# Weight transfers of one unit in five buffers, and the low part of a unit in one operation

## The chip, the cores and the metric

The kernel runs on one core of a Trainium2 chip. The metric is the device time of one execution in microseconds. The kernel before took 2624.03 us, the median of three runs (2620.69 to 2626.52).

## The reference

Two layers of a hybrid block over 256 tokens of width 2048, in float32. In each layer, with `h` the residual stream:

```python
u = rms_norm(h, mix_pre_g[l])
proj = u @ w_in[l]                        # 2048 x 4352, in layer 1 also w_in_vres
y_rwkv = rwkv7_time_mix(...)              # 16 heads of 64, a scan over the tokens
y_mla = mla_heads(...)                    # 8 heads, w_uq (512 x 1536), w_ukv (256 x 2048)
y = concatenate([y_rwkv, y_mla]) @ w_out[l]
h = h + rms_norm(y, mix_post_g[l])
y = memory_cross_attention(rms_norm(h, mem_pre_g[l]), mem_n, wq, wk, wv, wo)
h = h + rms_norm(y, mem_post_g[l])
y = square(relu(rms_norm(h, ffn_pre_g[l]) @ w_ff1[l])) @ w_ff2[l]   # 2048 x 8192 and back
h = h + rms_norm(y, ffn_post_g[l])
```

Every weight is used once for all 256 tokens, so each one passes from HBM to the core once.

## The kernel before

Matmuls with the big weights take both operands as a high and a low part: the high part is the value cast to TensorE's 32-bit matmul format (fp32r), the low part is the value minus the high part. A product is three matmuls: high x high, high x low, low x high (`go`, L309, and the same in `gemmB`, L360).

A *unit* is the piece of a weight that is split at once: 512 KB for 512 columns, two k-tiles of 128 rows (`per = 2`), or four k-tiles for up to 256 columns (`per = 4`). Its way has these steps:

1. **Transfer.** SP's queue issues the transfer from HBM into a tile of the pool `rawp` (L148), which has two buffers. `units` (L258) takes two units in one transfer of up to 1 MB. `hunits` (L280), for the weights of the attention projections, where columns of several heads are picked out, takes a whole slice of 2 or 4 k-tiles into one buffer, one transfer of 256 KB for each k-tile. A buffer comes free when the low parts of all its units are done, and SP issues its transfers in order.
2. **High part.** ScalarE casts the unit (L298), into a ring of four buffers (`ring`, L149), or, where `heap` says so, into the larger pool `heap4`.
3. **Low part.** VectorE subtracts (L300 or L304). While `ffn_on` is set (the two FFNs, from the second of their eight blocks of hidden columns on) this is one operation for a unit (L300); elsewhere it is two, one for each half of the unit's k-tiles (L304).
4. **Use.** TensorE reads both. A ring buffer comes free after its last matmul.

The first units of all (`first`, in the small projection of layer 0) are an exception: the first two have a transfer and a buffer in `heap4` each, and the pairs in `rawp` begin after them.

The matmul loops take the units from generators: `gemmA` (tokens as the stationary operand, weights moving) and `gemmB` (weights stationary) are one unit ahead of TensorE in the program, `gemm_seq` follows an order that is written out. The last product of each FFN goes through `gemm_seq`: all units of the third column block for the first 128 tokens, then the same units for the other 128, then the fourth block in the same way, whose units are split into `heap4`.

TensorE's order is the program's own: between the matmuls of the big products, small generators (`spawn`, `poll`, `wait`) add the matmuls of the scan, of attention and of the transposes, by a running clock with fixed delays. The other engines' queues are ordered by the planner of the framework, which also sets all semaphores. So a cast for a weight stands in ScalarE's queue between copies from PSUM, squares and exponentials, and a subtraction in VectorE's between the operations of the scan.

Names in the profile: `raw` is a transferred tile, `wh` and `wl` the two parts, `uh`/`ul` the split activations, `hdh`/`hdl` the hidden layer of the FFN, `qn`, `kn`, `qrT` copies in the attention projections, `rf` and `rl` the FFN's activations.

Of the kernel before, what the change touches and what calls it, by code (L numbers as in the profile page):

```python
# [9 lines left out]
F32 = mybir.dt.float32  # L10
F32R = mybir.dt.float32r
AF = mybir.ActivationFunctionType
ALU = mybir.AluOpType
# [3 lines left out]
NK = 16  # L17
# [116 lines left out]
class K:  # L134
# [1 line left out]

    def __init__(self, tc, I, out, ctx, n4=24, n2=18, nring=4, nraw=2):
        self.tc, self.nc, self.I, self.out = tc, tc.nc, I, out  # L140
        self.n = 0
        self.clk, self.fib, self.evt = 0.0, [], {}
        E = ctx.enter_context
        PS = bass.MemoryType.PSUM
        self.cp = E(tc.tile_pool(name="cp", bufs=1))
        self.heap = E(tc.tile_pool(name="heap", bufs=n2))
        self.heap4 = E(tc.tile_pool(name="heap4", bufs=n4))
        self.rawp = E(tc.tile_pool(name="rawp", bufs=nraw))  # L148
        self.ring = E(tc.tile_pool(name="ring", bufs=nring))  # L149
        self.tp = E(tc.tile_pool(name="tp", bufs=8))  # L150
        self.sp = E(tc.tile_pool(name="sp", bufs=16))
        self.gp = E(tc.tile_pool(name="gps", bufs=4, space=PS))
        self.xp = E(tc.tile_pool(name="xps", bufs=4, space=PS))
        self.dr = E(tc.tile_pool(name="drp", bufs=1, space=bass.MemoryType.DRAM))
        nc = self.nc
        self.Id = self.cp.tile([128, 128], F32, name="Id")
        self.V = self.cp.tile([128, L, NV], F32, name="V")
        self.C = self.cp.tile([128, NC_ - 128], F32, name="C")
        self.mhalf = self.cp.tile([128, 16], F32, name="mhalf")
        nc.gpsimd.memset(self.mhalf, -0.5)  # L160
        self.ident = self.Id
# [93 lines left out]
        g.tensor_tensor(out=dst, in0=t, in1=self.mhalf[:, : src.shape[-1]], op=ALU.pow)  # L255


    def units(self, src, k0, nk, ncols, extra=None, heap=None, first=False):  # L258

        nc = self.nc  # L260
        per = 4 if ncols <= 256 else 2
        ks = range(k0, k0 + nk, 2 * per)
        if first:
            ks = [k0, k0 + per, *ks[1:]]
        for ka, kb in zip(ks, [*ks[1:], k0 + nk]):
            kn = kb - ka
            if first and kn == per:
                raw = self.t4("raw", [128, kn, ncols])
            else:
                raw = self.rawp.tile([128, kn, ncols], F32, tag="raw", name=self.nm("raw"))  # L270
            rows = slice(ka * 128, (ka + kn) * 128)
            n0 = src.shape[1]
            nc.sync.dma_start(out=raw[:, :, :n0], in_=src[rows, :].rearrange("(k p) n -> p k n", p=128))
            if extra is not None:
                nc.sync.dma_start(out=raw[:, :, n0:], in_=extra[rows, :].rearrange("(k p) n -> p k n", p=128))
            for j in range(0, kn, per):
                i = (ka + j - k0) // per
                yield self.split(raw[:, j : j + per, :], per, ncols, heap is not None and i >= heap) + (list(range(ka + j, ka + j + per)),)

    def hunits(self, w, nk, h0, nh, dh, hw, off):  # L280

        nc = self.nc
        raw = self.rawp.tile([128, nk, nh, dh], F32, tag="raw", name=self.nm("raw"))
        wv = w.rearrange("(k p) (h c) -> k p h c", p=128, c=hw)
        for k in range(nk):
            nc.sync.dma_start(out=raw[:, k], in_=wv[k, :, h0 : h0 + nh, off : off + dh])
        rv = raw.rearrange("p k h d -> p k (h d)")
        for j in range(0, nk, 2):
            yield self.split(rv[:, j : j + 2, :], 2, nh * dh) + ([j, j + 1],)

    def split(self, raw, per, ncols, heap=False):
        nc = self.nc
        if heap:
            wh, wl = (self.t4(s, [128, per, ncols], F32R) for s in ("wh", "wl"))
        else:
            wh = self.ring.tile([128, per, ncols], F32R, tag="wh", name=self.nm("wh"))
            wl = self.ring.tile([128, per, ncols], F32R, tag="wl", name=self.nm("wl"))
        nc.scalar.copy(out=wh, in_=raw)  # L298
        if self.ffn_on:
            nc.vector.tensor_tensor(out=wl, in0=raw, in1=wh.bitcast(F32), op=ALU.subtract)  # L300
        else:
            for j in range(0, per, per // 2):
                s = slice(j, j + per // 2)
                nc.vector.tensor_tensor(out=wl[:, s], in0=raw[:, s], in1=wh[:, s].bitcast(F32), op=ALU.subtract)  # L304
        return wh, wl

    ffn_on = False

    def go(self, o, x, wh, wl, start, stop):  # L309
        xh, xl = x  # L310
# [222 lines left out]

    def small_units(self, l):
        w = self.I["w_in"][l]
        return self.units(w[:, 3072:3520], 0, NK, 448 + (64 if l else 0), extra=self.I["w_in_vres"][l - 1] if l else None, heap=4, first=l == 0)

    def small(self, l, U, rstd, units):
        nc, I = self.nc, self.I
# [803 lines left out]
    def ffn(self, l, U, rstd, done, ff):  # L1343
        nc, I = self.nc, self.I
        w1, w2 = I["w_ff1"][l], I["w_ff2"][l]
        rhs = self.rhsU(U)
        y = None
        part = [self.sm("fp", [128, 4]) for _ in range(2)]
        gb = None
        NB = 8  # L1350

        def ff1(b):
            H = ([], [])
            for j in range(2):
                hh, hl = self.newU(4, "hd")
                c0 = b * 1024 + j * 512
                if b == 0 and j == 0:
                    self.ff1_first(l, ff, U, hh[0], hl[0])
                else:
                    def ev(q, ps, hh=hh[0], hl=hl[0]):  # L1360
                        r = self.t2("rl", [128, 2, 256])
                        nc.scalar.activation(out=r, in_=ps, func=AF.Relu)  # L1362
                        nc.gpsimd.tensor_tensor(out=r, in0=r, in1=r, op=ALU.mult)  # L1363
                        o = hh[:, 2 * q : 2 * q + 2, :]
                        nc.scalar.copy(out=o, in_=r)  # L1365
                        nc.vector.tensor_tensor(out=hl[:, 2 * q : 2 * q + 2, :], in0=r, in1=o.bitcast(F32), op=ALU.subtract)  # L1366

                    self.gemmB(self.units(w1[:, c0 : c0 + 512], 0, NK, 512), NK, rhs, ev)
                H[0].extend(hh)
                H[1].extend(hl)  # L1370
            return H

        def ff2(b, H, gb):
            lh = self.lhsU(H)
            lhs = lambda k, t: lh(k - 8 * b, t)

            def ev(n):
                def f(t, ps):
                    o = y[t][n]
                    if b == 0:  # L1380
                        nc.scalar.activation(out=o, in_=ps, func=AF.Copy, scale=s2[t])
                    else:
                        nc.vector.scalar_tensor_tensor(out=o, in0=ps, scalar=s2[t], in1=o, op0=ALU.mult, op1=ALU.add)  # L1383
                    if b == NB - 1:
                        junk = self.t2("junk", [128, 512])
                        nc.scalar.activation(out=junk, in_=o, func=AF.Square, accum_out=part[t][:, n : n + 1])
                        y[t][n] = self.t2("yg", [128, 512])
                        nc.vector.tensor_tensor(out=y[t][n], in0=o, in1=gb[n], op=ALU.mult)
                        if n == 3:
                            done(t, y, part)  # L1390
                return f

            un = lambda n, heap=None: self.units(w2[:, n * 512 : (n + 1) * 512], 8 * b, 8, 512, heap=heap)
            last = b == NB - 1
            for n in range(2 if last else 4):
                self.gemmA([un(n)], 8, lhs, 512, ev(n))
            if last:
                self.gemm_seq([(un(2), 8, 512, ev(2)), (un(3, 0), 8, 512, ev(3))], lhs,
                              [(0, 0, 4), (0, 1, 4), (1, 0, 4), (1, 1, 4)])

        H = ff1(0)
        y = self.tiles4()
        s2 = [self.sm("s2", [128, 1]) for _ in range(2)]
        for t in range(2):
            nc.gpsimd.tensor_tensor(out=s2[t], in0=rstd[t], in1=rstd[t], op=ALU.mult)
        self.ffn_on = True
        for b in range(NB):
            Hn = ff1(b + 1) if b + 1 < NB else None
            if b == NB - 1:
                gb = self.load_bc(I["ffn_post_g"][l])  # L1410
            ff2(b, H, gb)
            H = Hn
        self.ffn_on = False


    def load_h(self, h, src, q, t, cols=range(4)):
# [100 lines left out]
```

## Time and profile before

| | before |
|---|---|
| median of 3 runs, us | 2624.03 |
| profiled execution, us | 2620.89 |
| its span, us | 2619.1 |
| granted TensorE clock, mean | 0.989 |
| TensorE matmuls busy, us | 2528.3 (97%) |
| VectorE busy, us | 1593.2 (61%) |
| ScalarE busy, us | 1205.2 (46%) |
| GpSimd busy, us | 435.4 (17%) |
| moved by DMA | 456.69 MB, 174 GB/s in the mean |

The span goes from the first to the last instruction. A matmul's end is modelled, and matmuls overlap, so TensorE counts as busy while any of them is under way. "Idle before, releaser" in a row is the time for which an engine did nothing before an instruction, and what ended that. L273 and the like are lines of the kernel; PE is TensorE, DVE VectorE, ACT ScalarE, POOL GpSimd, SP the queue that issues the weights' transfers. PEclk is the granted TensorE clock as a share of full speed.

In time the span has: the start and the mixing stage of layer 0 (projections, scan, attention, w_out) to about 445 us, memory attention to about 570, the FFN to about 1300, then the same for layer 1.

### The profile page before, as it was taken

To read this page: it belongs to the slowest core of one execution; us is meant where nothing else is said; L and a number is where in the kernel's file an instruction comes from. 1 tells how busy PE (TensorE), PEld (TensorE's weight loads), DVE (VectorE), ACT (ScalarE), POOL (GpSimd) and SP (SyncE) were. 2 spreads that over 40 slices of the span, in tenths; PEclk is the share of its full clock that TensorE was granted. 3 is DMA by queue.
4 is the path that set the end of the run, shared out by engine and by line. 5 is a ranking of instruction groups with operands and counts; after the bars stand their busy time and mean duration, and the time that the engine had idled before them with its cause. 6 is when DMAs were issued, how large, how long until landed. Compare 5 with 4: busy or idle time off the path is not lost.

```text
span 2619.1 us, 42411 instructions
## 1 busy us (share of the span) xinstructions
PE 2528.3 (97%) x17458; PEld 2280.7 (87%) x17458; DVE 1593.2 (61%) x2445; ACT 1205.2 (46%) x1724; POOL 435.4 (17%) x597
## 2 busy tenths in 40 slices
PE   8999999999999999999999998999999999999997
PEld 7989878979899899989788887789798998899896
DVE  4786876675445555555667778757754545555555
ACT  5454555544444444444454544545544444444443
POOL 2323414211000000000034245202100000000000
PEclk9999999999999999999999999999999999999999
DMA  5444536645555555555554444365455555555554
GB/s 201 153 150 132 156 123 207 206 129 178 192 181 190 193 188 183 191 195 193 194 167 154 143 132 149 114 233 190 129 177 193 182 189 193 186 184 193 188 198 145
DMA packets 250850, 456.69 MB, mean 174 GB/s; under 512 B 19268, under 2 KB 52420, under 8 KB 250656
## 3 DMA queue, kind: packets, MB, share of 16 engines
q1 hardware_dynamic: 241280, 422.77, 49.3%
q0 software_dynamic: 9376, 31.21, 3.6%
q8 instruction: 137, 2.24, 0.4%
q14 instruction: 57, 0.47, 0.1%
HBM read 444.50 MB, written 9.44 MB: 173 GB/s over the span
## 4 chain that ended last, share of the span: by engine, by line
PE 65%; issue 12%; DVE 10%; DMA 7%; ACT 3%; POOL 3%; SPq 0%; ACTq 0%; DVEq 0%; POOLq 0%
PE g L243 57%; PE x L243 7%; DVE wl L304 3%; DMA raw<-in_w_ff_dram 2%; ACT wh L298 2%; DMA raw<-in_w_in_dram 1%; PE x L248 1%; DMA raw<-in_w_out_dram 1%; DVE h L469 1%; DVE wl L300 1%; DVE uf L411 1%; DMA raw<-in_wk_mem_dram 1%; DMA raw<-in_wq_mem_dram 1%; DVE T L784 0%; DVE fs L782 0%
## 5 line engine op out<-in xcount | busy, mean ns | idle before, releaser
L298 ACT CAST wh<-raw 128x1024 fp32r<-128x1024 f32 (+2 forms) x804 | 832.0, 1042 | 1043.3 <-PE g L243 690.4
L300 DVE TENSOR_TENSOR wl<-raw,wh 128x1024 fp32r<-128x1024 f32 x480 | 586.1, 1223 | 570.7 <-ACT wh L298 567.8
L243 PE MATMUL g<-uh,wh 128*128 128x256 f32 x2816 | 807.1, 287 | 0.7 <-ACT wh L298 0.7
L243 PE MATMUL g<-uh,wl 128*128 128x256 f32 x2816 | 796.9, 283 | 1.2 <-DVE wl L304 1.2
L243 PE MATMUL g<-ul,wh 128*128 128x256 f32 x2816 | 796.6, 283 | 0.0
L304 DVE TENSOR_TENSOR wl<-raw,wh 128x512 fp32r<-128x512 f32 (+2 forms) x648 | 433.0, 709 | 193.1 <-ACT wh L298 192.2
L243 PEld LDWEIGHTS g<-uh,wh 128*128 128x128 f32 x2816 | 539.9, 192 | 6.2 <-issue 2.3
L243 PEld LDWEIGHTS g<-uh,wl 128*128 128x128 f32 x2816 | 540.2, 192 | 4.2 <-DVE wl L304 2.0
L243 PEld LDWEIGHTS g<-ul,wh 128*128 128x128 f32 x2816 | 540.0, 192 | 0.0
L243 PE MATMUL g<-wh,hdh 128*128 128x512 f32 x1024 | 399.4, 390 | 3.1 <-ACT wh L298 3.1
L243 PE MATMUL g<-wl,hdh 128*128 128x512 f32 x1024 | 399.7, 390 | 1.5 <-DVE wl L300 1.5
L243 PE MATMUL g<-wh,hdl 128*128 128x512 f32 x1024 | 398.9, 390 | 0.0
L1363 POOL TENSOR_TENSOR rl<-rl 128x512 f32<-128x512 f32 x60 | 61.3, 1041 | 1174.4 <-ACT rl L1362 1174.3
L243 PEld LDWEIGHTS g<-wh,hdh 128*128 128x128 f32 x1024 | 192.6, 188 | 43.5 <-ACT wh L298 3.9
L243 PEld LDWEIGHTS g<-wl,hdh 128*128 128x128 f32 x1024 | 192.7, 188 | 42.1 <-DVE wl L300 2.8
L243 PEld LDWEIGHTS g<-wh,hdl 128*128 128x128 f32 x1024 | 192.7, 188 | 40.1
L243 PE MATMUL g<-wh,uh 128*128 128x256 f32 (+3 forms) x320 | 113.2, 354 | 13.1 <-ACT wh L298 7.0
L243 PE MATMUL g<-wl,uh 128*128 128x256 f32 (+3 forms) x320 | 110.0, 344 | 10.2 <-DVE wl L304 10.0
L243 PE MATMUL g<-wh,ul 128*128 128x256 f32 (+3 forms) x320 | 108.5, 339 | 2.5 <-POOL ul L413 1.7
L1366 DVE TENSOR_TENSOR hdl<-rl,hdh 128x512 fp32r<-128x512 f32 x60 | 47.7, 795 | 67.6 <-ACT hdh L1365 67.6
L1383 DVE SCALAR_TENSOR_TENSOR y<-g,s,y 128x512 f32<-128x512 f32 x112 | 78.9, 743 | 9.0 <-PE g L243 9.0
L243 PEld LDWEIGHTS g<-wh,uh 128*128 128x128 f32 x320 | 62.4, 195 | 19.9 <-ACT wh L298 8.3
(342 smaller groups left out, 3042.4 us busy)
## 6 DMA issues: line engine op xcount, KB each, us to landing
raw<-in_w_ff_dram SPq DMA_DIRECT2D x256, 1024.0 KB, 5.3
raw<-in_w_in_dram SPq DMA_DIRECT2D x56, 1024.0 KB, 5.3
raw<-in_w_out_dram SPq DMA_DIRECT2D x32, 1024.0 KB, 5.1
raw<-in_wk_mem_dram SPq DMA_DIRECT2D x8, 1024.0 KB, 5.4
raw<-in_wq_mem_dram SPq DMA_DIRECT2D x8, 1024.0 KB, 6.5
raw<-in_wv_mem_dram SPq DMA_DIRECT2D x8, 1024.0 KB, 5.3
raw<-in_wo_mem_dram SPq DMA_DIRECT2D x8, 1024.0 KB, 5.0
raw<-in_w_in_dram SPq DMA_DIRECT2D x7, 896.0 KB, 5.2
```

What stands on the lines that cost most here:

```text
L243: return self.nc.tensor.matmul(out, lhsT, rhs, start=start, stop=stop, skip_group_check=skip)
L248: self.nc.tensor.transpose(out, in_, self.ident[p0 : p0 + n, p0 : p0 + n])
L298: nc.scalar.copy(out=wh, in_=raw)
L300: nc.vector.tensor_tensor(out=wl, in0=raw, in1=wh.bitcast(F32), op=ALU.subtract)
L304: nc.vector.tensor_tensor(out=wl[:, s], in0=raw[:, s], in1=wh[:, s].bitcast(F32), op=ALU.subtract)
L411: nc.vector.tensor_tensor(out=u, in0=p, in1=gain[:, 4 * j : 4 * j + nk].unsqueeze(2).to_broadcast([128, nk, 128]), op=ALU.mult)
L469: nc.vector.scalar_tensor_tensor(out=h[t][c], in0=y[t][c], scalar=rs, in1=h[t][c], op0=ALU.mult, op1=ALU.add)
L1363: nc.gpsimd.tensor_tensor(out=r, in0=r, in1=r, op=ALU.mult)
L1366: nc.vector.tensor_tensor(out=hl[:, 2 * q : 2 * q + 2, :], in0=r, in1=o.bitcast(F32), op=ALU.subtract)
L1383: nc.vector.scalar_tensor_tensor(out=o, in0=ps, scalar=s2[t], in1=o, op0=ALU.mult, op1=ALU.add)
```

## The change

`rawp` has five buffers instead of two, and each holds one unit: `units` and `hunits` both issue the transfers of one unit into a new buffer and split it. The case for the first units (`first`) goes. The low part is one operation everywhere, and `ffn_on` goes. In `units` a transfer of 1 MB becomes two of 512 KB; in `hunits` the transfers stay at 256 KB, but two k-tiles share a buffer instead of two or four. The cast, the ring and the matmuls are as before, and TensorE's order is the same.

```diff
-    def __init__(self, tc, I, out, ctx, n4=24, n2=18, nring=4, nraw=2):
+    def __init__(self, tc, I, out, ctx, n4=24, n2=18, nring=4, nraw=5):
...
-    def units(self, src, k0, nk, ncols, extra=None, heap=None, first=False):
+    def units(self, src, k0, nk, ncols, extra=None, heap=None):
 
         nc = self.nc
         per = 4 if ncols <= 256 else 2
-        ks = range(k0, k0 + nk, 2 * per)
-        if first:
-            ks = [k0, k0 + per, *ks[1:]]
-        for ka, kb in zip(ks, [*ks[1:], k0 + nk]):
-            kn = kb - ka
-            if first and kn == per:
-                raw = self.t4("raw", [128, kn, ncols])
-            else:
-                raw = self.rawp.tile([128, kn, ncols], F32, tag="raw", name=self.nm("raw"))
-            rows = slice(ka * 128, (ka + kn) * 128)
-            n0 = src.shape[1]
+        n0 = src.shape[1]
+        for i in range(nk // per):
+            ka = k0 + i * per
+            raw = self.raw(per, ncols)
+            rows = slice(ka * 128, (ka + per) * 128)
             nc.sync.dma_start(out=raw[:, :, :n0], in_=src[rows, :].rearrange("(k p) n -> p k n", p=128))
             if extra is not None:
                 nc.sync.dma_start(out=raw[:, :, n0:], in_=extra[rows, :].rearrange("(k p) n -> p k n", p=128))
-            for j in range(0, kn, per):
-                i = (ka + j - k0) // per
-                yield self.split(raw[:, j : j + per, :], per, ncols, heap is not None and i >= heap) + (list(range(ka + j, ka + j + per)),)
+            yield self.split(raw, per, ncols, heap is not None and i >= heap) + (list(range(ka, ka + per)),)
 
     def hunits(self, w, nk, h0, nh, dh, hw, off):
 
         nc = self.nc
-        raw = self.rawp.tile([128, nk, nh, dh], F32, tag="raw", name=self.nm("raw"))
         wv = w.rearrange("(k p) (h c) -> k p h c", p=128, c=hw)
-        for k in range(nk):
-            nc.sync.dma_start(out=raw[:, k], in_=wv[k, :, h0 : h0 + nh, off : off + dh])
-        rv = raw.rearrange("p k h d -> p k (h d)")
         for j in range(0, nk, 2):
-            yield self.split(rv[:, j : j + 2, :], 2, nh * dh) + ([j, j + 1],)
+            raw = self.raw(2, nh * dh)
+            for k in range(2):
+                nc.sync.dma_start(out=raw[:, k].rearrange("p (h d) -> p h d", d=dh), in_=wv[j + k, :, h0 : h0 + nh, off : off + dh])
+            yield self.split(raw, 2, nh * dh) + ([j, j + 1],)
+
+    def raw(self, per, ncols):
+        return self.rawp.tile([128, per, ncols], F32, tag="raw", name=self.nm("raw"))
...
         nc.scalar.copy(out=wh, in_=raw)
-        if self.ffn_on:
-            nc.vector.tensor_tensor(out=wl, in0=raw, in1=wh.bitcast(F32), op=ALU.subtract)
-        else:
-            for j in range(0, per, per // 2):
-                s = slice(j, j + per // 2)
-                nc.vector.tensor_tensor(out=wl[:, s], in0=raw[:, s], in1=wh[:, s].bitcast(F32), op=ALU.subtract)
+        nc.vector.tensor_tensor(out=wl, in0=raw, in1=wh.bitcast(F32), op=ALU.subtract)
         return wh, wl
-
-    ffn_on = False
...
-        ... heap=4, first=l == 0)
+        ... heap=4)
```

## Rows read from the trace of the kernel before

**Rows 1.** Engines of the page: busy us, share of the span, instructions.
```profile
PE 2528.3 (97%) x17458; PEld 2280.7 (87%) x17458; DVE 1593.2 (61%) x2445; ACT 1205.2 (46%) x1724; POOL 435.4 (17%) x597
```
**Rows 2.** Span and mean granted clock of the core.
```profile
core 0: 2619.1 us, clock 0.989
```
**Rows 3.** Stretches: length, PE, PEld, DVE, ACT, POOL busy, PEclk, DMA share, GB/s.
```profile
650.00:700.00 50.00, 50.00 (x340) 46.55 (x339) 24.26 (x22) 24.24 (x28) 4.08 (x4) 1.00 0.55 186
...
2560.00:2585.00 25.00, 25.00 (x112) 20.71 (x111) 16.77 (x19) 13.27 (x19) 0.00 (x0) 1.00 0.59 200
10.00:15.00 5.00, 0.06 (x1) 0.00 (x0) 1.55 (x4) 2.79 (x8) 4.58 (x10) 1.00 1.06 390
...
1600.00:1650.00 50.00, 37.85 (x244) 32.87 (x243) 42.60 (x123) 25.80 (x48) 19.18 (x26) 0.97 0.52 169
```
**Rows 4.** Waits of TensorE, whole span: us in total, times, longest us.
```profile
PE g L243 <- DVE wl L304: 14.5, 20, 3.1
PE g L243 <- ACT wh L298: 10.8, 6, 6.1
...
PE g L243 <- ACT qn L1099: 6.2, 2, 3.7
PE g L243 <- ACT uh L412: 6.1, 3, 2.5
PE x L243 <- ACT qrT L1063: 5.4, 2, 3.2
...
PE g L243 <- DVE wl L300: 1.5, 2, 0.8
```
**Rows 5.** Chain that ended last, 2500 to 2600: start us, us, what.
```profile
2585.81 4.99 DMA raw<-in_w_ff_dram
```
**Rows 6.** Timeline of TensorE, 2586 to 2596: start us, us, instruction [idle before].
```profile
2591.92 0.50 PE L243 MATMUL g<-wh,hdh 128*128 128x512 f32 x1 [1.55 <-ACT wh L298]
2593.18 0.50 PE L243 MATMUL g<-wl,hdh 128*128 128x512 f32 x1 [0.76 <-DVE wl L300]
```
**Rows 7.** DMA issues of the page: times, KB each, median us to landing.
```profile
raw<-in_w_ff_dram SPq DMA_DIRECT2D x256, 1024.0 KB, 5.3
```
**Rows 8.** SP's issues of tile raw: ns min/median/max, first and last.
```profile
L273 SPq DMA_DIRECT2D raw<-in_w_ff_dram x256: 367/368/368, 560.8 to 2585.8; - x128
```
**Rows 9.** Timeline of ScalarE, layer 1's attention projections, 1575 to 1655.
```profile
1625.46 1.05 ACT L298 CAST wh<-raw 128x1024 fp32r<-128x1024 f32 x1 [6.56 <-DMA raw<-in_w_ukv_dram]
1626.41 0.58 ACT L1063 COPY qrT<-x 128x512 f32<-128x512 f32 x1
...
1635.28 1.05 ACT L298 CAST wh<-raw 128x1024 fp32r<-128x1024 f32 x1 [7.32 <-DMA raw<-in_w_out_dram]
```
**Rows 10.** Timeline of SP's queue, the same stretch.
```profile
1619.08 0.93 SPq L286 DMA_DIRECT2D raw<-in_w_ukv_dram  x2
```
**Rows 11.** Timeline of ScalarE, 0 to 31.
```profile
12.87 0.19 ACT L389 ACTIVATION_READ_ACCUMULATOR junk<-h 128x1 f32 x1
15.15 5.14 ACT L298 CAST wh<-raw 128x896 fp32r<-128x896 f32 x6 [2.10 <-DMA raw<-in_w_in_dram]
```
**Rows 12.** DMA issues, 0 to 30: times, KB each, median us to landing.
```profile
raw<-in_w_in_dram SPq DMA_DIRECT2D x3, 896.0 KB, 7.9
...
raw<-in_w_in_dram SPq DMA_DIRECT2D x2, 448.0 KB, 10.5
```
**Rows 13.** Waits of TensorE, 465 to 482, then 155 to 180.
```profile
PE g L243 <- DVE wl L304: 3.4, 2, 2.5
...
PE g L243 <- DVE wl L304: 1.7, 2, 1.2
```
**Rows 14.** Stretch after it, TensorE alone: length, busy, PEclk, DMA share, GB/s.
```profile
478.00:485.00 7.00, 6.81 (x45) 0.74 0.80 276
```
**Rows 15.** Costliest groups of the page, VectorE: busy us, mean ns, idle before.
```profile
L300 DVE TENSOR_TENSOR wl<-raw,wh 128x1024 fp32r<-128x1024 f32 x480 | 586.1, 1223 | 570.7 <-ACT wh L298 567.8
...
L304 DVE TENSOR_TENSOR wl<-raw,wh 128x512 fp32r<-128x512 f32 (+2 forms) x648 | 433.0, 709 | 193.1 <-ACT wh L298 192.2
```
**Rows 16.** Timeline of VectorE, 540 to 600.
```profile
558.20 4.90 DVE L304 TENSOR_TENSOR wl<-raw,wh 128x512 fp32r<-128x512 f32 x8 [0.24 <-ACT wh L298]
```

More of the change, by code (lines that the diff above doesn't have):

```diff
@@ L295, in split @@
         else:
-            wh = self.ring.tile([128, per, ncols], F32R, tag="wh", name=self.nm("wh"))
-            wl = self.ring.tile([128, per, ncols], F32R, tag="wl", name=self.nm("wl"))
+            wh, wl = (self.ring.tile([128, per, ncols], F32R, tag=s, name=self.nm(s)) for s in ("wh", "wl"))
         nc.scalar.copy(out=wh, in_=raw)
-        if self.ffn_on:
-            nc.vector.tensor_tensor(out=wl, in0=raw, in1=wh.bitcast(F32), op=ALU.subtract)
-        else:
-            for j in range(0, per, per // 2):
-                s = slice(j, j + per // 2)
-                nc.vector.tensor_tensor(out=wl[:, s], in0=raw[:, s], in1=wh[:, s].bitcast(F32), op=ALU.subtract)
+        nc.vector.tensor_tensor(out=wl, in0=raw, in1=wh.bitcast(F32), op=ALU.subtract)
         return wh, wl
-    ffn_on = False
     def go(self, o, x, wh, wl, start, stop):
@@ L535, in small_units @@
         w = self.I["w_in"][l]
-        return self.units(w[:, 3072:3520], 0, NK, 448 + (64 if l else 0), extra=self.I["w_in_vres"][l - 1] if l else None, heap=4, first=l == 0)
+        return self.units(w[:, 3072:3520], 0, NK, 448 + (64 if l else 0), extra=self.I["w_in_vres"][l - 1] if l else None, heap=4)
     def small(self, l, U, rstd, units):
@@ L1405, in ffn @@
             nc.gpsimd.tensor_tensor(out=s2[t], in0=rstd[t], in1=rstd[t], op=ALU.mult)
-        self.ffn_on = True
         for b in range(NB):
@@ L1412, in ffn @@
             H = Hn
-        self.ffn_on = False
     def load_h(self, h, src, q, t, cols=range(4)):
```

## The prediction

> **What bounds the kernel now.** I read the page's engine shares first. TensorE is busy 2528.3 of 2619.1 us [rows 1], so the room is 90.8 us of its idle time and what a lower granted clock costs, at most (1 - 0.989) x 2619 = 29 us [rows 2]. Next come the sums by stretch [rows 3]: in the middle of the FFN TensorE is busy 50.00 of 50.00 us at clock 1.00, in the second layer's attention part 37.85 of 50. So feeding TensorE faster gains nothing in the body of the two FFNs and has to win around them. Third, the list of what TensorE waited for [rows 4]: the low part of a weight unit (L304) 14.5 us in 20 waits, its high part (L298) 10.8 us in 6; then evacuations and casts that share ScalarE's queue with the weight casts: qn 6.2, uh 6.1, qrT 5.4 us. With the 1.5 us on L300 these rows make 44.5 us; that is what the change can reach. Fourth, the chain and the timelines at these places, to see whether a transfer, VectorE or the order of a queue made the weights late.
>
> The profiled execution took 2620.9 us, 1.8 more than its span and 3.1 less than the median of the three runs, 2624.0. I sum against 2620.9 and add the 3.1 at the end.
>
> **The change part by part.**
>
> *Five buffers of one unit, FFN.* A unit of the second FFN product is 12 matmuls (2 k-tiles, 2 token tiles, 3 products). Near the last FFN's end TensorE did 112 in 25 us [rows 3], so a unit lasts it 12 x 0.223 = 2.68 us. There the chain is a ring: a 1 MB transfer waits until both units of its buffer are done, takes 5 us [rows 5], then come cast and subtraction, and the next transfer has waited again. At the end TensorE stood 1.55 us for the high part and 0.76 us for the low part of a late unit [rows 6]; the first layer has the like (L300 has 1.5 us in two waits, [rows 4]). With five buffers, one goes around in landing + cast + subtraction + issue. Even if 512 KB landed no sooner than 1 MB does (5.3 us, [rows 7]), that is 5.3 + 1.05 + 1.22 + 0.37 = 7.9 us (cast, low part and issue from [rows 9], [rows 15] and [rows 8]) for five units, 1.6 us each, against 2.68 wanted. I take the waits at both ends as gone: 2 x 2.31 = -4.6 us; at worst they stay, 0. Elsewhere in the FFN nothing moves: TensorE is never idle there, and the low part is one operation already.
>
> *The same, attention projections.* Here `hunits` gave a two-unit buffer to a whole weight slice, even to one of a single unit. In the second layer the last w_ukv slice was issued only at 1619.08 [rows 10]; ScalarE waited 6.56 us for it until 1625.46, and the second qrT copy, next in the same queue, came at 1626.41; the next cast waited 7.32 us for w_out [rows 9]. So TensorE's waits for qrT (5.4 us) and qn (6.2 us) [rows 4] stand behind late transfers. Five buffers let these leave several units sooner. What is late next is VectorE, busy 42.60 of 50 us there [rows 3], so I take three quarters of 11.6: -8.7. Bounds: 0 and -11.6.
>
> *Start.* The first cast of a weight began at 15.15, 2.10 us after ScalarE had finished its squares at 13.06 [rows 11]. The 448 KB units landed 10.5 us after their issue (median), the larger ones, issued about the same time, after 7.9 [rows 12]: the first two units, which have buffers of their own, came last. If the first unit now goes first, ScalarE's queue is the limit: -2.1. If the order stays, 0; if the cast also goes ahead of the squares, up to -6.1, the longest wait on L298 [rows 4].
>
> *Other late units.* In the memory keys TensorE waited 3.4 us for low parts, in the 320-column units 1.7 us [rows 13]. VectorE had other work queued at both, so I take half of 5.1: -2.5, with 0 and -5.1 as ends. After the first, the clock was 0.74 on average from 478 to 485 [rows 14], so part of that stretch was at the lower level, 1.2 GHz, and it lost 0.26 x 7 = 1.8 us. For this and the like I take -2.0 (0 to -29).
>
> *Casts of uh at the start of each FFN*, 6.1 us [rows 4]: they wait for VectorE's residual work, which stands behind subtractions of late units. A third: -2.0 (0 to -6.1).
>
> *Low part as one operation.* 648 halves, outside the FFN and in its first block, become 324 operations [rows 15]. Eight halves back to back took 4.90 us [rows 16], so a pair takes 1.29 us, its first half 0.69; a whole one takes 1.22 [rows 15]. VectorE saves 0.07 us a unit, 23 us in all, most of it beside TensorE's work. Against that, TensorE's second matmul needs the first half only, and where it stands waiting gets it 1.22 - 0.69 = 0.53 us later. Of the 20 such waits [rows 4] I count 8 as first halves that the prefetch doesn't remove: +4.3. Bounds: all 20, +10.6; below zero, VectorE's saving ends half of the 14.5 us, -7.
>
> *SP's queue.* 256 transfers of 1 MB in the FFN [rows 7] and some 135 elsewhere become twice as many: 391 x 0.37 us [rows 8] = 145 us more for a queue that mostly waits for free buffers, 0.37 in each 2.68 us. 0. Losing the two separate buffers at the start (five units in flight, not six) is 0 as well while TensorE waits for the first.
>
> Sum: -4.6 - 8.7 - 2.1 - 2.5 - 2.0 - 2.0 + 4.3 = -17.6. 2620.9 - 17.6 + 3.1 = 2606.4, so 2606.
>
> **A rule against it.** From 10 to 15 us, with transfers of 256 to 1024 KB under way together, the core moved 390 GB/s [rows 3]; 512 KB each 2.68 us is 196 GB/s. The Trainium skill, "DMA: Bandwidth & Descriptors", section "Bandwidth", says to batch to 1 MiB or more for three quarters of peak; with the fixed cost of some 2.0 us that the same page gives, a lone 512 KB transfer would take about 3.2 us (an estimate by that page), more than a unit lasts, and the FFN would get slower. The row speaks against that here: transfers under way together hide each other's fixed time.
>
> **The rivals.**
>
> *A. The waits change owner.* TensorE's order outside the FFN is written out with fixed delays, and what it gains it loses again at the next VectorE or GpSimd chain. For it: VectorE's 42.60 of 50 us [rows 3]. Against it: the waits for qrT and qn begin at a transfer. Then the FFN ends, the start and the price of one operation stay: -4.6 - 2.1 + 4.3 = -2.4, 2621.6.
>
> *B. Slower, by the one operation.* In the scan and attention stages the low parts stand between chains of short VectorE operations; one that is 0.53 us longer delays first matmuls and those chains. The place is every unit outside the FFN, the price 0.53 us for each that TensorE feels, and it decides from (17.6 + 4.3) / 0.53 = 41 of the 324 units, against 20 waits now. With a quarter of them, 81, it is +42.9 - 21.9 = +21.0: 2645. Against it: a ring of four ready units lies between VectorE and TensorE.
>
> *C. Small transfers don't overlap.* If 512 KB units came one after the other, each in 4.0 us (between half of the 5.3 us of 1 MB and all of it), FFN units would take 4.0 instead of 2.68 us; over some 1200 us that is +590, 3214. The 390 GB/s speak against it.
>
> *D. The transfers leave no sooner.* A planner, not the code's order, sets the queues of SP, ScalarE and VectorE; at the start now the units wanted first landed last [rows 12]. Then the gains are about as small as the price of one operation: 2624.
>
> **How the numbers follow.** Forecast 0.58, A 0.22, B 0.15, C 0.01, D 0.04. A measurement of this kernel can tell about 0.2%, 5.2 us, from no change. The forecast is all faster; A, spread some us about 2621.6, is 0.06 faster, 0.14 same, 0.02 slower; B and C are slower; D is 0.02 same, 0.02 slower. Together faster 0.64, same 0.16, slower 0.20. The forecast's own range is 2588 to 2617: its low end has all waits gone (-4.6 - 11.6 - 6.1 - 5.1 - 2.0 - 6.1 = -35.5, with one operation at 0), its high end half of every gain (-10.9 + 4.3 = -6.6). The range for 8 in 10 takes in A, D and the cheap part of B: 2588 to 2632.
>
> **What would show it.** Right: no wait of TensorE at the two FFN ends; casts in the attention projections without 6 and 7 us for w_ukv and w_out, and waits for qrT and qn under 1 us each; first weight cast near 13 us; waits on low parts of about 0.5 us where there were none. Wrong: FFN stretches with TensorE under 50 of 50 (C), waits on low parts above 25 us (B), as much idle time as now under other names (A), or w_ukv issued as late as now (D).

## The result and the profile after

The changed kernel takes 2588.23 us (median of 4 runs, 2587.36 to 2589.59) against 2623.03 (4 runs, 2620.69 to 2626.52): ratio 0.9867, 95% interval 0.985 to 0.9884, so 34.8 us less, where the forecast was 17. The time lies at the very low end of the forecast's range (2588 to 2617). The direction held; the size was half, and which part of the change makes the gain came out otherwise than the sum had it.

The page's engines and the core, as in [rows 1] and [rows 2]:

```profile
PE 2524.0 (98%) x17458; PEld 2285.7 (88%) x17458; DVE 1557.1 (60%) x2121; ACT 1209.3 (47%) x1724; POOL 444.6 (17%) x597
```

```profile
core 0: 2586.8 us, clock 0.987
```

TensorE's idle time fell from 90.8 to 2586.8 - 2524.0 = 62.8 us, 28.0 less. VectorE has 324 instructions fewer, the halves that went. What TensorE waited for, as in [rows 4]:

```profile
PE g L243 <- ACT uh L398: 7.9, 5, 2.0
PE g L243 <- ACT qn L1085: 6.4, 2, 3.5
...
PE g L243 <- DVE wl L292: 4.7, 8, 1.6
PE g L243 <- ACT wh L291: 4.3, 2, 3.2
```

Low and high parts of weights cost 9.0 us instead of 26.8 (14.5 + 10.8 + 1.5); qrT, 5.4 before, has no row any more; qn and uh stand as they were or a little higher.

The stretches that answer to [rows 3], in another order, and those near the end some 28 to 32 us earlier; columns as there:

```profile
10.00:15.00 5.00, 2.93 (x9) 1.96 (x8) 4.61 (x5) 4.61 (x8) 4.72 (x8) 1.00 1.05 393
650.00:700.00 50.00, 50.00 (x257) 42.89 (x256) 23.43 (x20) 25.11 (x29) 2.04 (x2) 1.00 0.60 190
2528.00:2553.00 25.00, 25.00 (x112) 20.68 (x112) 17.00 (x18) 13.12 (x16) 0.00 (x0) 1.00 0.60 200
1572.00:1622.00 50.00, 42.08 (x258) 37.16 (x258) 41.83 (x110) 26.94 (x49) 23.61 (x28) 0.93 0.44 135
```

The FFN body is as full as before. In the second layer's attention TensorE works 42.08 of 50 us instead of 37.85. Beside [rows 7], a unit's transfer in the FFN lands after 4.2 us, where 1 MB took 5.3:

```profile
raw<-in_w_ff_dram SPq DMA_DIRECT2D x512, 512.0 KB, 4.2
```

Both kernels give TensorE the same 17458 matmuls in the same order, so the start of each can be compared with its counterpart's. The difference in start at a stage's border, after minus before, says what the stages up to there won; its change over a stage is that stage's part. With the terms of the forecast (us, one profiled execution each):

| stage, by the time before | after - before at its end | this stage | forecast |
|---|---|---|---|
| start, to 51 | -4.4 | -4.4 | -2.1 |
| layer 0 projections and scan, to 271 | -8.4 | -4.0 | -0.8 (320-column units) |
| layer 0 attention, w_out, to 451 | -11.7 | -3.3 | -8.7 with layer 1 |
| layer 0 memory attention, to 548 | -19.2 | -7.5 | -3.7 with layer 1 (late units 1.7, clock 2.0) |
| FFN entry, to 606 | -21.2 | -2.0 | -2.0 with layer 1 |
| FFN body, to 1251 | -21.2 | 0.0 | 0 |
| FFN end, start of layer 1, to 1327 | -22.8 | -1.6 | -2.3 |
| layer 1 projections and scan, to 1571 | -23.4 | -0.6 | 0 |
| layer 1 attention, to 1713 | -27.3 | -3.9 | (above) |
| layer 1 memory attention, to 1847 | -28.6 | -1.3 | (above) |
| FFN entry, to 1907 | -29.9 | -1.3 | (above) |
| FFN body, to 2545 | -29.9 | 0.0 | 0 |
| FFN end, to 2606 | -32.4 | -2.5 | -2.3 |
| one operation, in all stages | | in the above | +4.3 |

### The profile page after: what moved, and what is told of

It is laid out like the page before. It is cut to its first block, busy times and chain, and to the rows that moved or that the text cites. A ratio compares the mean times of both kernels' runs of the same rounds, so it can differ in the third digit from the quotient of the medians.

```text
span 2586.8 us, 43201 instructions
## 1 busy us (share of the span) xinstructions
PE 2524.0 (98%) x17458; PEld 2285.7 (88%) x17458; DVE 1557.1 (60%) x2121; ACT 1209.3 (47%) x1724; POOL 444.6 (17%) x597
## 4 chain that ended last, share of the span: by engine, by line
PE 86%; DVE 6%; POOL 2%; issue 2%; DMA 1%; ACT 1%; SPq 0%; DVEq 0%; POOLq 0%; ACTq 0%
PE g L243 77%; PE x L243 7%; DVE wl L292 2%; PE x L248 2%; DVE fs L768 1%; DVE T L770 1%; DVE h L455 1%; DMA raw<-in_w_ff_dram 1%; ACT wh L291 1%; DMA vf<-vfirst 0%; DMA raw<-in_w_in_dram 0%; POOL yd L471 0%; POOL rsn L617 0%; POOL kT L837 0%; POOL vf L814 0%
## 5 line engine op out<-in xcount | busy, mean ns | idle before, releaser
L292 DVE TENSOR_TENSOR wl<-raw,wh 128x1024 fp32r<-128x1024 f32 (+2 forms) x804 | 978.1, 1222 | 736.9 <-ACT wh L291 733.3
L243 PE MATMUL g<-wh,uh 128*128 128x256 f32 (+3 forms) x320 | 114.6, 358 | 12.2 <-ACT uh L398 7.9
L1369 DVE SCALAR_TENSOR_TENSOR y<-g,s,y 128x512 f32<-128x512 f32 x112 | 79.0, 744 | 10.6 <-PE g L243 10.6
L243 PEld LDWEIGHTS g<-wl,uh 128*128 128x128 f32 x320 | 63.9, 200 | 9.6 <-DVE wl L292 5.9
```

The costliest lines, as they stand in the source:

```text
L243: return self.nc.tensor.matmul(out, lhsT, rhs, start=start, stop=stop, skip_group_check=skip)
```

## The experiments

Theory: the gain is transfers that leave and land sooner, and each of its sources can be had by itself: the landing of a unit by itself (512 KB, not 1 MB), a buffer for each unit, the start's order. Rivals: a fifth buffer or the one operation makes it; or the waits depend on each other and nothing adds up. Ratios are to the kernel before on the same chip, with 95% intervals. The last six columns give the difference in start to the kernel before at some borders of the table above, one profiled execution for each kernel.

| kernel | median us | ratio | at 51 | 271 | 451 | 548 | 1713 | end |
|---|---|---|---|---|---|---|---|---|
| after | 2588.23 | 0.9867 (0.985 to 0.9884) | -4.4 | -8.4 | -11.7 | -19.2 | -27.3 | -32.4 |
| after, halves kept | 2590.0 | 0.9881 (0.9868 to 0.9895) | -3.0 | -7.3 | -10.5 | -18.1 | -29.8 | -34.0 |
| after, four buffers | 2587.03 | 0.9872 (0.9857 to 0.9887) | -4.8 | -8.3 | -11.6 | -19.2 | -28.3 | -34.4 |
| after, three buffers | 2605.38 | 0.9947 (0.9934 to 0.996) | 2.0 | -0.6 | -4.8 | -12.2 | -12.1 | -14.7 |
| three buffers, ring of five | 2607.54 | 0.9952 (0.994 to 0.9965) | 1.2 | -2.8 | -3.6 | -11.1 | -9.6 | -13.3 |
| after, two buffers | 2888.04 | 1.1016 (1.0997 to 1.1035) | 5.1 | 13.8 | 20.7 | 32.9 | 148.9 | 268.8 |
| after, qn on VectorE | 2591.26 | 0.9886 (0.9872 to 0.99) | -5.1 | -8.7 | -11.1 | -18.7 | -23.7 | -30.4 |
| before, small transfers in pairs | 2600.99 | 0.9928 (0.9915 to 0.9941) | 0.2 | -2.5 | -3.0 | -10.6 | -17.0 | -21.7 |
| the same, no own buffers at the start | 2598.36 | 0.9917 (0.9903 to 0.9932) | -0.9 | -3.4 | -3.7 | -10.8 | -15.5 | -18.7 |
| before, pairs in memory attention only | 2614.87 | 0.9974 (0.9962 to 0.9985) | 0.4 | 0.3 | -0.2 | -7.3 | -4.8 | -4.5 |
| before, no own buffers at the start | 2620.92 | 1.0 (0.999 to 1.0009) | -0.7 | -1.0 | -0.1 | -3.9 | -4.2 | -4.7 |
| before, one operation | 2623.64 | 1.0011 (1.0 to 1.0023) | 1.9 | -0.3 | -4.4 | -5.6 | 4.3 | 4.5 |

The old kernel with small edits differs from itself by some us from stage to stage (the last two rows), so a difference under some 4 us is read only where a view shows the wait behind it.

**The low part.** The changed kernel with the halves back outside the FFN, and the kernel before with one operation everywhere:

```diff
-        nc.vector.tensor_tensor(out=wl, in0=raw, in1=wh.bitcast(F32), op=ALU.subtract)
+        if self.ffn_on: ...      # one operation, else one for each half, as before
```

> The changed kernel with its five one-unit buffers, but the low part in two halves outside the FFN, as before. Theory 1 (the forecast's sum: the buffers bring everything, one operation costs 4.3 us): 4 us faster than the changed kernel, about 2584. Theory 2 (the one operation itself brings the part that the forecast lacked, by taking work off VectorE at the FFN entries, where TensorE waited 2.1 us for low parts in each layer before and not after): 5 to 15 us slower than the changed kernel, 2593 to 2603, with those waits back.

> The kernel before with the low part as one operation everywhere, its two 1 MB buffers kept. Theory 1: 4 us slower than before, about 2627. Theory 2: 5 to 15 us faster than before, 2608 to 2618, and no waits on low parts at 587 to 595 us.

With the new buffers the halves make no difference that can be told: 2590.0 against 2588.23, and the intervals of the ratios overlap; both theories missed. In the old kernel the one operation alone costs between 0 and 0.23%, 0 to 6 us: the 4.3 of the forecast is not excluded there, nor is nothing. What decides TensorE's waits for low parts is the transfers and their buffers, not the number of operations. With the halves and the new buffers, then with one operation and the old buffers:

```profile
PE g L243 <- DVE wl L297: 5.4, 4, 3.0
```

```profile
PE g L243 <- DVE wl L299: 14.3, 16, 2.3
```

Against 4.7 us after and 14.5 before, neither differs much.

**How many buffers.** `nraw` from 5 to 4, 3 and 2, and 3 with a deeper ring:

```diff
-nring=4, nraw=5
+nring=4, nraw=4      # and 3, and 2; and nring=5, nraw=3
```

> The changed kernel with four one-unit buffers, the same bytes as the two of 1 MB before. If what counts is that a buffer comes free for each unit (granularity), it keeps most of the gain: 2588 to 2595. If it is the depth (the fifth unit), it loses half or more: 2605 and above.

> The changed kernel with three one-unit buffers. The ring's arithmetic gives 6.8 / 3 = 2.3 us a unit, under the 2.68 to 2.88 us of TensorE, so no loss in the FFN's body, but no reserve to catch up after a late unit: 2590 to 2600. If depth counts beyond the arithmetic: above 2605.

> The changed kernel with three one-unit buffers and a ring of five units (the same bytes as five and four). If what is left of TensorE's waits for low parts and high parts (9 us in the changed kernel) comes from the ring's depth, 3 to 8 us faster than the changed kernel, 2580 to 2585. If it comes from late transfers or from the order of queues, as with three buffers alone, 2588 to 2600.

> The changed kernel with two one-unit buffers. By the ring's arithmetic (4.2 landing + 1.05 cast + 1.22 low part + 0.37 issue = 6.8 us for two units, 3.4 us each, against 2.68 to 2.88 us that TensorE takes): 0.6 us for each of some 480 units in the FFN, about 290 us, and the rest slower too: 2850 to 2950. If transfers are not what limits a ring of few buffers: under 2620.

Four buffers, the bytes that the pool had before, keep the whole gain: the fifth is worth nothing that can be told. With two the kernel is as slow as expected, and the FFN is bound by the ring of transfers, as the forecast's arithmetic has it: (landing 3.6 + cast 1.05 + low part 1.22 + issue 0.37) / 2 = 3.12 us a unit against the 2.68 that TensorE takes; the first FFN body took 645.2 + 73.6 us, so a unit took 2.68 x 718.8 / 645.2 = 2.99, some 4% under the arithmetic. TensorE's waits with two buffers, then the landing:

```profile
PE g L243 <- DVE wl L292: 105.7, 170, 5.6
PE g L243 <- ACT wh L291: 33.7, 42, 3.3
```

```profile
raw<-in_w_ff_dram SPq DMA_DIRECT2D x512, 512.0 KB, 3.6
```

With three it is (4.1 + 2.64) / 3 = 2.25 us, and the FFN bodies lose nothing; yet 17 us of the gain are gone: some 6 at the start, and most of the rest from the end of the first FFN through layer 1's scan. So depth counts beyond the arithmetic, as the second theory had it; TensorE's waits for low parts are 16.7 us in 16, not 4.7 in 8. With three buffers the ring of ready units is not what is short: five of them bring nothing (2607.54, outside both ranges). That three buffers have no reserve after a stop fits this, but was not tried by itself.

**The landing alone.** The kernel before, its two-unit buffers kept, each transfer of 1 MB issued as two of 512 KB:

```diff
+            for j in range(0, kn, per):
+                part = src[(ka + j) * 128 : (ka + j + per) * 128, :]
-            nc.sync.dma_start(out=raw[:, :, :n0], in_=src[rows, :]....)
+                nc.sync.dma_start(out=raw[:, j : j + per, :n0], in_=part....)
```

> The kernel before with each 1 MB transfer issued as two of 512 KB into the halves of the same two-unit buffer (the buffer still comes free as a whole). If the gain is the sooner landing of the first unit (4.2 instead of 5.3 us, so about 1 us at each late transfer), it is 5 to 12 us faster than before, 2611 to 2618. If it is that the transfer can be issued sooner, because its buffer comes free alone, it is within 3 us of before.

This gives 18.9 us (0.72%, 0.59 to 0.85), over half of the whole gain and more than any theory gave it, with no buffer added and each still freed as a whole. Both theories missed; what is left is that the first unit of a pair need not wait for the second. Transfers in the FFN landed after 4.5 us (median), not 5.3. What it lacks against four buffers of one unit (2587.03) is at the start, 5.0 us, and some 3 us in each of the two attention stages, where its waits for qrT stand as before (5.9 us).

**The memory keys.** The largest stage by itself, the same edit for three weights only:

```diff
-        self.gemmB(self.units(I["wk_mem"][l], 0, NK, 512), ...)
+        self.gemmB(self.units(I["wk_mem"][l], 0, NK, 512, step=2), ...)    # also wq_mem, wv_mem
```

> The kernel before with the transfers of 1 MB as two of 512 KB only for the three weights of the memory attention (keys, queries, values). Theory 1 (the gain at the memory keys comes from the first half of a pair landing sooner there, and does not need an earlier lead of the kernel): 7 to 8 us less at the end of layer 0's memory attention, about 1 in layer 1, the whole 2613 to 2617 us. Theory 2 (the waits there depend on what the stages before left): 0 to 3 us less in layer 0, the whole 2618 to 2624.

In the profiled execution the stage wins 7.1 us (from -0.2 to -7.3), as in the whole change; by the medians the kernel wins 5.9 us (0.26%, 0.15 to 0.38). So the first theory holds: the gain needs no lead from the stages before. (Some 3 us of it are given back later, in layer 1's mixing stage, in the profiled execution.) The stretch from 451 to 485, first in the kernel before, then with this edit, then in the kernel before without the separate buffers at the start, which changes nothing here (columns as in [rows 3]):

```profile
451.00:485.00 34.00, 30.54 (x189) 27.87 (x188) 21.46 (x35) 11.47 (x17) 9.21 (x13) 0.90 0.75 251
```

```profile
451.00:485.00 34.00, 33.88 (x244) 31.61 (x243) 26.86 (x43) 16.73 (x24) 13.21 (x16) 1.00 0.71 254
```

```profile
451.00:485.00 34.00, 32.60 (x235) 30.43 (x234) 25.64 (x40) 15.48 (x22) 12.20 (x16) 1.00 0.73 256
```

As many GB/s, but with the edit TensorE does 244 matmuls instead of 189, at clock 1.00 instead of 0.90. The third line is a caution: with the old transfers this execution waits 1.4 us, not 3.4, keeps clock 1.00, and is through the stage 3.8 us sooner than the kernel before. So the profiled execution of before is a bad case of this stage, and about half of the 7.1 us comes and goes with the execution. The medians are the better measure.

**The start.** No separate buffers for the first units: in the kernel before, and with the small transfers in pairs:

```diff
-        return self.units(..., heap=4, first=l == 0)
+        return self.units(..., heap=4)
```

> The kernel before without the exception for the first units: at the start too, two units share a 1 MB transfer and a buffer. In the changed kernel TensorE's first weight matmul came 4.3 us sooner than before. Theory 1: that comes from the exception's going, because the units wanted first were issued last; then 3 to 4 us faster than before, 2618 to 2619, first weight cast before 13.1 us. Theory 2: it needs transfers of one unit, since the first 896 KB land later than the first 448 KB; then the start gains 1.5 us at most and the time is that of before.

> The kernel before with each transfer of 1 MB as two of 512 KB into the same two-unit buffer, and without the two separate buffers for the first units. Theory 1 (what counts at the start is that the first unit is issued first and lands by itself as 512 KB; either edit alone gave nothing there because the other half was missing): the first weight matmul and the ones up to 50 us come 3 to 5 us sooner than before, the whole 2594 to 2599 us, 22 to 26 less than before. Theory 2 (the start needs more buffers, so that the third and fourth units leave at once): the first weight matmul comes sooner but nothing of it is left at 50 us, and the whole is 2599 to 2603, as with the small transfers alone.

The first weight matmul came 3.5 and 4.6 us sooner, but at 51 us only 0.7 and 0.9 are left; with small transfers and no separate buffers the whole is 2598.36: that lies just inside the first theory's range, but it can't be told from 2600.99 (the intervals of the ratios overlap), and the start lost its lead as the second theory said. So the start needs a buffer for each unit, and more than three: with three the kernel is 2.0 us later at 51 than before. SP's queue shows why. Its issues (start us, us, what), after, then with the pairs and no separate buffers:

```profile
3.58 2.96 SPq L267 DMA_DIRECT2D raw<-in_w_in_dram  x4
...
10.89 6.17 SPq L267 DMA_DIRECT2D raw<-in_w_in_dram  x4
```

```profile
3.57 2.68 SPq L275 DMA_DIRECT2D raw<-in_w_in_dram  x4
...
16.13 3.02 SPq L275 DMA_DIRECT2D raw<-in_w_in_dram  x4
```

Four units leave at once in both; the next group leaves at 10.89 there and at 16.13 here, when both units of the first pair are done (at 13.58 with four buffers of one unit). TensorE then stands at 20.73 here:

```profile
20.73 0.47 PE L243 MATMUL g<-wh,uh 128*128 128x448 f32 x1 [1.50 <-ACT wh L300]
```

**The wait for qn.** In the changed kernel qn still costs 6.4 us. Its copies from PSUM were put on VectorE:

```diff
-                nc.scalar.copy(out=qn[:, 2 * b : 2 * b + 2, :], in_=ps)
+                nc.vector.tensor_copy(out=qn[:, 2 * b : 2 * b + 2, :], in_=ps)
```

> The changed kernel with the copies of qn from PSUM on VectorE, not ScalarE. Theory 1 (qn is late since its copy stands behind exponentials that wait for VectorE's maxima, and no transfer is involved): TensorE's 6.4 us on qn become under 2 us, the whole 2582 to 2586, 2 to 6 less than the changed kernel. Theory 2 (VectorE's queue of attention and scan chains is the late one, and its queue delays the copy as much): qn waits as long or the maxima come later, the whole 2587 to 2592.

The second theory holds: 2591.26, its ratio's interval overlapping that of the changed kernel, and TensorE's waits by name:

```profile
PE g L243 <- DVE qn L1085: 6.8, 3, 3.7
```

The wait has another owner and another place (the longest, 3.73 us, is in layer 1 at 1600.08, before the w_ukv product). Nothing is gained; how to end it stays open.

## Why the forecast had the sign and half the size

The step that failed: the sum asked of each wait what more buffers would free, and weighed it by the engine that it was named after. No term has a unit that lands by itself (the FFN term takes 5.3 us for 512 KB as for 1 MB). That alone, in the two old buffers, made 18.9 us, more than the 17.6 of the whole sum. What it cost is seen best in *Other late units* below; and +4.3 us was charged for the one operation, where nothing is felt.

**FFN ends, -4.6: right in size, but not by the ring of five.** Of the two waits of [rows 6] one short one is left:

```profile
2556.76 0.50 PE L243 MATMUL g<-wl,hdh 128*128 128x512 f32 x1 [0.21 <-DVE wl L292]
```

The stages around the two ends won 1.6 + 2.5 = 4.1 us. The two old buffers with small transfers won 3.7 + 1.9 us there, so what was needed is the sooner landing, not a fifth buffer. The first end by itself won 4.1 us (to -25.3 at 1300), and the start of layer 1 gives 2.5 back. Before, TensorE waited there for the low part of a unit:

```profile
1320.81 0.50 PE L243 MATMUL g<-wl,uh 128*128 128x512 f32 x1 [3.07 <-DVE wl L304]
```

After, it waits 3.23 us for the high part of the same unit and then 0.69 for its low part. The unit left in time, but its cast stands in ScalarE's queue behind one of uh that waits 4.76 us for VectorE (ScalarE, then TensorE, after):

```profile
1294.32 0.62 ACT L398 CAST uh<-uf 128x512 fp32r<-128x512 f32 x1 [4.76 <-DVE uf L397]
1294.84 2.93 ACT L291 CAST wh<-raw 128x1024 fp32r<-128x1024 f32 x3
```

```profile
1295.93 0.80 PE L243 MATMUL g<-wh,uh 128*128 128x512 f32 x1 [3.23 <-ACT wh L291]
```

SP had issued that weight's first units from 1279.84 to 1284.50. This is rival A in one place: the wait changes owner.

**Attention projections, -8.7: near in size (-7.2), which is in part luck, and wrong in one half of the argument.** The waits for qrT (5.4 us) ended, and w_out leaves at 1584.33 instead of 1626.36 (some 23 of these 42 us are the lead of the stages before):

```profile
1584.33 26.06 SPq L267 DMA_DIRECT2D raw<-in_w_out_dram  x6
```

But the 6.2 us of qn, counted in, gave nothing (6.4 after): a transfer was not all that held it. With every cast early, ScalarE still idles until VectorE has the softmax's maxima (nm), 7.24 us in layer 0 and 8.37 in layer 1, and the qn copy is behind those exponentials:

```profile
313.40 0.37 ACT L1120 ACTIVATE pr<-x,nm 128x128 f32<-128x128 f32 x1 [7.24 <-DVE nm L1117]
...
319.25 1.07 ACT L1085 COPY qn<-g 128x512 f32<-128x512 f32 x2
...
1608.91 0.37 ACT L1120 ACTIVATE pr<-x,nm 128x128 f32<-128x128 f32 x1 [8.37 <-DVE nm L1117]
```

The waits of 6.56 and 7.32 us in [rows 9] were real, and behind them stood a second limit of the same length.

**Other late units, -2.5, and clock, -2.0: the step that failed most.** The memory attention of both layers won 8.8 us in the profiled executions where I had 3.7 (small transfers there alone: 5.9 by the medians). I halved the waits of [rows 13] since VectorE had other work queued. It had, but that work was late itself. The trace of before at that place; ScalarE, then VectorE (the low part at 473.40 is the one for which TensorE waits 2.53 us, to 474.14):

```profile
466.65 1.05 ACT L298 CAST wh<-raw 128x1024 fp32r<-128x1024 f32 x1 [4.45 <-DMA raw<-in_wk_mem_dram]
```

```profile
467.74 1.29 DVE L304 TENSOR_TENSOR wl<-raw,wh 128x512 fp32r<-128x512 f32 x2 [4.99 <-ACT wh L298]
...
470.68 2.74 DVE L469 SCALAR_TENSOR_TENSOR h<-y,prs,h 128x512 f32<-128x512 f32 x4 [0.39 <-POOL prs L255]
...
473.40 0.68 DVE L304 TENSOR_TENSOR wl<-raw,wh 128x512 fp32r<-128x512 f32 x1
```

VectorE stood idle for the cast of the unit before, and that cast for its transfer. The residual work (h) that stands before the late low part came right behind that unit in VectorE's queue. With small transfers in the memory attention alone, VectorE does the same operations in the same order 5.3 us sooner, and TensorE has no wait there:

```profile
468.08 0.68 DVE L307 TENSOR_TENSOR wl<-raw,wh 128x512 fp32r<-128x512 f32 x1
```

After, all eight units of the keys leave from 433.59 on, in time (SP):

```profile
433.59 17.33 SPq L267 DMA_DIRECT2D raw<-in_wk_mem_dram  x8
```

The first name in a list of waits (low part, VectorE) was the last link of a chain that began at a DMA. I also priced the lower clock by the 7 us of [rows 14], 1.8 us; over the 34 us above it cost 0.10 x 34 = 3.4 us, and with the wait gone it is 1.00. Not all of this is owed to the change, since with 1.4 us of wait left it was 1.00 too (the third line under *The memory keys*).

**Casts of uh, -2.0: the size came, not the step.** The FFN entries won 2.0 + 1.3 us, but the waits for uh stand. At the first entry what went are five short waits for low parts; two lines of before, then after:

```profile
PE g L243 <- ACT uh L412: 3.6, 2, 2.5
PE g L243 <- DVE wl L304: 2.1, 5, 0.7
```

```profile
PE g L243 <- ACT uh L398: 3.5, 2, 2.0
```

**Start, -2.1: mis-sized, -4.4.** The cast does go ahead of the squares, the end of my bounds that I did not take:

```profile
10.90 0.94 ACT L291 CAST wh<-raw 128x896 fp32r<-128x896 f32 x1
```

**Projections and scan of layer 0, -4.0 where the sum had -0.8.** The difference in starts grows by 2.6 us between 125 and 136 us, where a stretch at the lower clock went; 20 us of before, then the same place after:

```profile
120.00:140.00 20.00, 17.39 (x98) 13.04 (x98) 16.99 (x33) 9.31 (x16) 8.27 (x15) 0.83 0.36 119
```

```profile
113.00:133.00 20.00, 17.46 (x121) 13.70 (x119) 19.25 (x34) 10.04 (x19) 8.28 (x15) 1.00 0.41 125
```

This too varies: with four buffers, and with qn on VectorE, the clock from 113 to 133 is 0.91, and yet these kernels win as much in the stage (3.5 and 3.6 us). How much of the 4.0 the change makes by the clock stays open.

**One operation, +4.3: mis-sized, about 0.** I counted 8 of the 20 waits of the old kernel as staying, each 0.53 us longer. Low parts are left with 8 waits of 4.7 us in all, but with the halves back nothing that can be told is won: a unit that is early enough is not waited for, and does not feel 0.53 us. Rival B needed 41 such units.

The differences, memory attention -5.1, one operation -4.3, projections and scans -3.8 (both layers), start -2.3, FFN entries -1.3, less 1.5 and 0.5 by which attention and FFN ends fell short, make the 14.8 us between -17.6 and the -32.4 of the profiled executions. They are differences of one execution each, so single stages are known to some 4 us at best.

**Rival C** did not come: a 512 KB transfer takes 4.2 us where a unit is used every 2.68, so more than one is under way, and the FFN bodies are as long as before. Halving the transfers alone made the kernel 0.72% faster, and 10 to 15 us moves 393 GB/s. The Trainium skill, "DMA: Bandwidth & Descriptors", section "Bandwidth", has the rule to batch transfers to 1 MiB or more for three quarters of peak bandwidth; here the smaller ones won, and the measurement decides. **Rival D** is out: SP's issues are earlier in every stage looked at.

## What to carry over

- A list of waits names the last link. Before a wait is discounted because its engine is busy, follow it back at its place: if that engine idled for a cast and the cast for a DMA, the whole wait can go.
- A price charged to waits of the old kernel (the one operation) must not be added in full beside a gain that removes these waits.
- Buffers are sized by (landing + processing + issue) / n against the consumer's time for a unit, plus a reserve that this does not size: here two fall short (+10%), three hold the steady stage but lose elsewhere, four give everything, a fifth nothing. Where memory is short, splitting the transfer inside the old buffer gives about half of the gain.

## What the runs showed of the hardware

A transfer of 512 KB landed after a median of 3.6 us with two buffers, 4.1 with three, 4.2 with five, against 5.3 for 1 MB before: half the size takes well over half the time, and what counts is that it can be used alone.

In the mean the clock shows neither gain nor loss, where I had counted a gain of 2.0 us. The four runs of the changed kernel have 0.987 to 0.989 (the profiled one 0.987), and the runs of the kernel before lie between 0.985 and 0.992, so no difference can be told. At the entry of the first FFN it did fall, before (571 to 591), then after:

```profile
571.00:591.00 20.00, 12.99 (x87) 10.39 (x85) 19.25 (x28) 9.19 (x17) 8.69 (x9) 1.00 0.21 62
```

```profile
550.00:570.00 20.00, 15.67 (x84) 13.88 (x83) 15.12 (x24) 6.95 (x12) 6.17 (x8) 0.74 0.25 77
```

With the waits for late low parts gone, TensorE's longer stops here are two for uh, 3.5 us, and its clock is 0.74 in the mean, so about half of the stretch at 1.2 GHz; before, with more idle time, it stayed at 1.00. The other profiled executions with four or five buffers have 0.74, 0.74 and 0.83 here, those of the old buffers 0.91 to 1.00, three buffers 0.91 (with the deeper ring 0.83). So at this entry the lower clock comes with the change and takes time back. At the second FFN's entry two of these four executions have no more of it than before. Why the clock falls here and not there these runs do not settle.
